# Pinned splits for late operands, one tile by token halves, and other places for the last products in a one-core encoder layer

## The chip, the core and the metric

The kernel runs on one core of a Trainium2 chip. The metric is device time in microseconds (us), the median of the runs shown. A core has five engines that matter here, each with its own instruction order: TensorE (PE; PEld is its weight load), VectorE (DVE), ScalarE (ACT), GpSimd (POOL) and SyncE (SP). SP and POOL issue DMAs; POOL's are those that add to what is in the target. Engines wait for each other through semaphores. A wait of one instruction holds everything behind it on its engine.

## The reference

One layer of an encoder, 1024 tokens by 1024 model columns in float32: a norm, a mixer (pooling and chunked attention), an output projection, a gated convolutional MLP with 2816 hidden columns, and a gated embedding. The change concerns the MLP and what follows it:

```python
    hn = rmsnorm(h, norm_ffn_g[i])
    up = hn @ w_up[i]
    gt, val = up[..., :D_FF], up[..., D_FF:]
    gt = causal_dwconv(gt, conv_w[i], conv_b[i])
    h = h + (jax.nn.gelu(gt, approximate=False) * val) @ w_down[i]
    hn = rmsnorm(h, norm_ple_g[i])
    gate = jax.nn.sigmoid(hn @ w_ple_gate[i] + b_ple_gate[i])
    h = h + gate * (p[i] @ w_ple[i])
return rmsnorm(h, final_g)
```

## The kernel before, in words

Every large product is made of three matmuls on split operands. `split` (L132) copies a 128x512 block on ACT into a reduced type (hi, L133) and subtracts that copy from the block on DVE (lo, L134); `mm3` (L126 to L130) then issues hi by hi (L128), hi by lo (L129) and lo by hi (L130).

*Up projection.* The 2816 hidden columns are 22 tiles `fi` of 128, each with a gate and a value column block. For each tile the two by two block product (gate and value columns by the two token halves) is done with seven products instead of eight, in a scheme of Strassen's kind. Product n of tile fi is written (fi,n) below; `product` makes it from 12 matmuls into a PSUM bank. The order is `steps`, n = 1, 5, 6, 2, 7, 3, 4 for most tiles; tiles 0 and 1 differ, and four products are run ahead, in the order (0,1), (1,1), (0,2), (0,5). `prepare` gets the weight operand of a product ready three products ahead: `fetch` (L695) loads w_up blocks (v,z) into one of six buffers, `summed` (L699) adds blocks on DVE where a product wants a sum, and `split` makes hi and lo. A buffer that a later sum has finished with goes to the next load, so which sums are made in place sets when loads can be issued. `step` does what follows a product: `keep` (L784) copies a bank to memory on ACT, `seed` (L788) copies one bank to another so that the next product can add to it, and DVE lines (L807 to L824) form gate and value. `gate` (L833 to L836) is the convolution and the gelu, `values_in` (L841 to L850) multiplies it by the value. A tile in `halved` has its gate done by token halves.

*Down projection.* Tiles 0 to 19 are stored to memory (L891, `Yd`), in groups of four tiles. For each of the five groups seven products (order 1, 2, 5, 4, 6, 7, 3; eight calls of `mm3`, 24 matmuls, each) are run in between up products. Their operands are sums of w_down blocks and of stored tiles; the DMA makes the sums: `ask` issues a plain load on SP (L942) and adding loads on POOL (L940) into the raw buffers RW, as far as the tiles that it needs are stored. `split_next` splits the four raw buffers (two of weights, two of activations; negative ones by L972 and L973) into the pair buffers, three of which are called BQ, and `down_next` runs the product and adds the banks to the residual (L990). `places` tells behind which up products of tile fi a down product runs.

*The last two tiles.* Tiles 20 and 21 are not stored; after tile 21 they go through a plain down product, with rows of w_down, and the embedding p and w_ple are multiplied as well. These late operands are loaded and split by `late_pair` (L1038), which has two buffers at first and six later.

The order of TensorE is that of the program. For ACT, DVE, SP and POOL a scheduler chooses the order from what is ready; `tc.high_priority(AHEAD)` lets an instruction go ahead by up to AHEAD places.

Of the kernel before, what the change touches and what calls it, by code (L numbers as in the profile page):

```python
# [12 lines left out]
SEQ = 1024  # L13
# [80 lines left out]
def trunk(tc, xT, pT, vecs, w_qk0, w_in, w_v, bias, counts, pool_w, w_out, w_up, w_down,  # L94
# [4 lines left out]
    with tc.tile_pool(name="sb", bufs=1) as sb, \  # L99
# [23 lines left out]
        def rv(ap):  # L123
            return ap.bitcast(F32)
# [4 lines left out]
            pe.matmul(ps, ahi, blo, start=False, stop=False, skip_group_check=more)  # L129
            pe.matmul(ps, alo, bhi, start=False, stop=last, skip_group_check=more)  # L130

        def split(src, hi, lo):  # L132
            act.activation(hi, src, AF.Copy)  # L133
            dve.tensor_tensor(lo, src, rv(hi), ALU.subtract)  # L134


        mhalf = small[:, 0:1]
# [530 lines left out]
        rst = f(44, SEQ)  # L668
        ahead = [(0, 1), (1, 1), (0, 2), (0, 5)]
        alone = ahead[:3]  # L670
        steps = {0: (6, 3, 7, 4), 1: (5, 6, 2, 7, 3, 4)}
        for fi in range(2, NF):
            steps[fi] = (1, 5, 6, 2, 7, 3, 4)
        order = ahead + [(fi, n) for fi in range(NF) for n in steps[fi]]
# [26 lines left out]
        def prepare(upto):  # L701
            while prepared[0] < min(upto, len(order)):
                fi, n = order[prepared[0]]
                w_ = wu[prepared[0] % 3]
                prepared[0] += 1
                fetch(prepared[0] + 3)
                assert fetched[0] == len(loads) or loads[fetched[0]][0] >= prepared[0]
                if (fi, n) in alone:
                    t, = done_with = [held[(fi, n), q] for q in FORMS[n]]
                else:  # L710
                    a11, a12, a21, a22 = [held.get((fi, q)) for q in ((0, 0), (0, 1), (1, 0), (1, 1))]
                    if n == 5:
                        summed(a21, a21, a22)
                    elif n == 6:
                        summed(a21, a21, a11)
                    elif n == 3 and not fi:
                        summed(a11, a21, a12)
                    elif n == 7:
                        if fi:
                            summed(a11, a21, a12)  # L720
                        summed(a21, a21, a22, ALU.subtract)
                    t = {1: a11, 5: a21, 2: a12, 6: a21, 3: a11, 7: a21, 4: a22}[n]
                    done_with = {3: [a11, a12], 7: [a21], 4: [a22]}.get(n, []) if fi == 0 else {
                        3: [a11], 7: [a12, a21], 4: [a22]}.get(n, [])
                with tc.high_priority(AHEAD):
                    split(rawu[t].rearrange("p (k c) -> p k c", k=4), w_[:, 0], w_[:, 1])
                for q in done_with:
                    used[q] = False
# [48 lines left out]
        p5, u2 = f(56.25, 512), f(58.25, 512)  # L777
        G2 = Gb[:, 2 + 512:2 + 1024]
        firsts = {0: (0, 3, 5, 4), 1: (2, 3, 1, 5)}
        halved = (1, NF - 1)  # L780

        def keep(dst, bank, scale=1.0):
            with tc.high_priority(AHEAD):
# [6 lines left out]
        def step(fi, n):  # L790

            x, y, z, w = firsts.get(fi, (0, 1, 2, 3))
            product({1: x, 2: x, 5: z, 3: z, 6: y, 7: y, 4: w}[n], n in (1, 5) or (fi, n) == (0, 4))
            if n == 1 and fi != 1:
                seed(y, x, -1.0)
            elif n == 2 and fi:
                gate0(x)
                if fi in halved:
                    gate(fi, HS[0])
            elif n == 5:  # L800
                keep(p5, z)
            elif n == 6:
                keep(u2, y)
            elif n == 3:
                if fi == 0:
                    norm_b.rows(rst[:, HS[1]])
                dve.tensor_tensor(G2, PS[:, z], u2, ALU.subtract)  # L807
                dve.tensor_tensor(G2, G2, rst[:, HS[1]], ALU.mult)
                gate(fi, HS[1] if fi in halved else slice(0, SEQ))
            elif n == 7:  # L810
                if fi:
                    seed(w, y)
                else:
                    keep(V[:, HS[0]], y)
                dve.tensor_tensor(V[:, HS[1]], PS[:, y], p5, ALU.subtract)
            elif n == 4:
                if fi:
                    dve.tensor_tensor(V[:, HS[0]], PS[:, w], rst[:, HS[0]], ALU.mult)
                else:
                    dve.tensor_tensor(V[:, HS[0]], PS[:, w], V[:, HS[0]], ALU.add)  # L820
                    dve.tensor_tensor(V[:, HS[0]], V[:, HS[0]], rst[:, HS[0]], ALU.mult)
# [16 lines left out]
        def values_in(ts, negative=None):  # L838
            b = max(ts.start, 512)
            if ts.stop > b:  # L840
                dve.tensor_tensor(V[:, b:ts.stop], V[:, b:ts.stop], rst[:, b:ts.stop], ALU.mult)  # L841
            if negative is None:
                dve.tensor_tensor(Yb[:, ts], Yb[:, ts], V[:, ts], ALU.mult)
                return
            for h in range(2):
                y = Yb[:, HS[h]]
                if h == negative:
                    dve.scalar_tensor_tensor(y, y, -1.0, V[:, HS[h]], ALU.mult, ALU.mult)
                else:
                    dve.tensor_tensor(y, y, V[:, HS[h]], ALU.mult)  # L850
# [26 lines left out]
        def up(fi, dst, hooks=None):  # L877
            if fi == 0:
                pool.memset(Gb[:, 0:2], 0.0)
                gate0(firsts[0][0])  # L880
            if fi == 1:
                seed(firsts[1][1], firsts[1][0], -1.0)
            for n in steps[fi]:
                step(fi, n)
                for hook in (hooks or {}).get(n, ()):
                    hook()
            if isinstance(dst, int):

                values_in(slice(0, SEQ), dst)
                for ts in HS:  # L890
                    sp.dma_start(Yd[fi][:, ts], Yb[:, ts])  # L891
                stored.add(fi)
                ask()
                if fi > 3:
                    split_next()
                return
            for ts in HS if fi % 2 else [slice(0, SEQ)]:
                values_in(ts)
                if dst is not None:
                    store(dst, ts)  # L900
# [19 lines left out]
        def ask():  # L920
# [3 lines left out]
            for side in "wa":  # L924
                for kind in ("one", "grow"):
                    queue = todo_of[side, kind]
                    while queue:
                        g, n, before = queue[0]
                        if before is not None and (side,) + before not in split_done:
                            break  # L930
                        if side == "a" and not all(group_of(g)[2 * k + j] in stored for k, _ in DOWN_A[n] for j in range(2)):
                            break
                        queue.pop(0)
                        asked.add((side, g, n))
                        grown = n in (GROWING_W if side == "w" else GROWING_A)[1:]
                        for j, srcs in sources(side, g, n):
                            t = raws[side, kind, j]
                            for z, src in enumerate(srcs):
                                if z or grown:
                                    pool.dma_start(t, src, accum_op=ALU.add)  # L940
                                else:
                                    sp.dma_start(t, src)  # L942
# [11 lines left out]
        sequence = [(g, n) for g in range(5) for n in DOWN_ORDER]  # L954
        nsplit, ndown = [0], [0]

        def split_next():
            if nsplit[0] == len(sequence) or nsplit[0] > ndown[0]:
                return
            g, n = sequence[nsplit[0]]  # L960
# [3 lines left out]
            for side in "wa":  # L964
                sign = -1.0 if side == "a" and n in NEGATIVE else 1.0
                for j in range(2):
                    t = raws[side, buffer(side, n), j]
                    hi, lo = pairs[side, j]
                    if sign > 0:
                        split(t, hi, lo)  # L970
                    else:
                        act.activation(hi, t, AF.Copy, scale=-1.0)  # L972
                        dve.scalar_tensor_tensor(lo, t, -1.0, rv(hi), ALU.mult, ALU.subtract)  # L973
# [26 lines left out]
        for fi in range(4):  # L1000
# [15 lines left out]
            if fi == 2:  # L1016
# [2 lines left out]
                                     (H[d][:, HS[1]], H[4 + d][:, HS[1]], ALU.add)):  # L1019
                        dve.tensor_tensor(a, a, b, op)  # L1020
                ask()
                split_next()
        places = [(1, 5), (2, 6), (3,), (0, 4)]
        for fi in range(4, NF - 3):
            up(fi, negative(fi), downs(fi, places[fi % 4]))
# [6 lines left out]
        pt = [[(r(b, 512), r(b + 2, 512)) for b in (96 + 16 * h, 104 + 16 * h)] for h in range(2)]  # L1032
        banks = (4, 5, 6, 7, 0, 2, 1, 3)
        nl = len(loads)
        late = [rawu[(nl + z) % 6] for z in (0, 1)]
        nlate = [0]

        def late_pair(src, hi, lo):  # L1038
            t = late[nlate[0] % len(late)]
            nlate[0] += 1  # L1040
            sp.dma_start(t, src)
            split(t, hi, lo)

        def ple_weights():
            for k in range(2):
                for z in HS:
                    late_pair(w_ple[k, :, z], wp[k][0][:, z], wp[k][1][:, z])

        def ple_rows(h):
            for k in range(2):  # L1050
                late_pair(pT[k, :, HS[h]], *pt[h][k])

        def down_weights(fi, dst):
            for z in HS:
                late_pair(w_down[fi, :, z], dst[0][:, z], dst[1][:, z])

        up(last_f[0], None, downs(last_f[0], (3, 5)))
        hooks = downs(last_f[1], (0, 2, 4, 6))
        for n, fn in ((1, lambda: store(gv2[0])), (2, ple_weights), (3, lambda: ple_rows(0)),
                      (4, lambda: late.extend(rawu[(nl + z) % 6] for z in (2, 3, 4, 5)))):  # L1060
            hooks.setdefault(n, []).insert(0, fn)
        up(last_f[1], gv2[1], hooks)
        b_pool.__exit__(None, None, None)
        b_pool = tc.tile_pool(name="po", bufs=1)
# [40 lines left out]
                mm3(PS[:, bank], wp[k][0][:, ds_], wp[k][1][:, ds_], *pt[h][k], k == 0, k == 1)  # L1105
            act.activation(po[8 * h + d], PS[:, bank], AF.Copy)

        down_weights(last_f[0], wd2[0])
        down_weights(last_f[1], wd2[1])
        ple_rows(1)  # L1110
        for d in range(KT):
            ple_mm(0, d, ple_banks[d])
        gate_weights(range(4))
# [164 lines left out]
```

## Time and profile before

| | us |
|---|---|
| runs | 1144.33, 1145.61, 1144.48 (median 1144.48) |
| profiled execution | 1146.88 |
| its span | 1145.1 |
| TensorE busy | 1129.9 |
| VectorE busy | 888.2 |
| ScalarE busy | 604.7 |
| GpSimd busy | 146.8 |

The mean granted clock of TensorE in the profiled execution is 0.995. The span is from the first to the last instruction of the profile. Matmuls overlap, so the time from one start to the next is what a matmul costs in a row; the duration in a timeline row is longer. In a row of the timeline the bracket gives the idle time ahead of the instruction and what ended it. "SPq" and "POOLq" are the queues of the engines that issue DMAs.

### The profile page before, as it was taken

How to read it: one execution, taken by the hardware profiler on the slowest of the kernel's cores; microseconds unless marked ns; L12 is line 12 of the kernel's file. 1: busy time of each engine (PE TensorE's matmuls, PEld its weight loads, DVE VectorE, ACT ScalarE, POOL GpSimd, SP SyncE). 2: the span in 40 equal slices, each digit the busy share in tenths (PEclk: the TensorE clock that was granted, in tenths of full speed). 3: DMA queues.
4: the chain of work that ended last, by engine and by line, in shares of the span. 5: the costliest groups of instructions: out<-in, count | busy, mean ns of one | idle time of the engine just before them, and what ended most of it. 6: DMA issues, size and time to landing. Idle time of an engine off the chain costs nothing.

```text
span 1145.1 us, 15750 instructions
## 1 busy us (share of the span) xinstructions
PE 1129.9 (99%) x5675; PEld 958.2 (84%) x5675; DVE 888.2 (78%) x1541; ACT 604.7 (53%) x1068; POOL 146.8 (13%) x192
## 2 busy tenths in 40 slices
PE   9999999999999999999999999999999999999997
PEld 7988998888888778888888888888888887788897
DVE  7678878879658787888787878777887788986864
ACT  8568677765554554444444444443444344664644
POOL 0000000073002200120112011201120113000000
PEclk9999999999999999999999999999999999999999
DMA  7110101104500343575557655755575559320012
GB/s 265 37 49 31 50 12 68 40 28 151 172 19 10 97 128 117 140 172 140 144 144 162 158 148 146 173 141 145 152 172 138 145 148 183 114 92 19 1 74 74
DMA packets 65022, 125.89 MB, mean 110 GB/s; under 512 B 7344, under 2 KB 8624, under 8 KB 64944
## 3 DMA queue, kind: packets, MB, share of 16 engines
q1 hardware_dynamic: 50400, 98.60, 25.9%
q0 software_dynamic: 14400, 26.22, 14.1%
q8 instruction: 44, 0.72, 0.3%
q14 instruction: 34, 0.28, 0.1%
q10 hardware_dynamic: 144, 0.07, 0.0%
HBM read 110.18 MB, written 14.68 MB: 109 GB/s over the span
## 4 chain that ended last, share of the span: by engine, by line
PE 93%; issue 2%; ACT 2%; DMA 1%; DVE 1%; SPq 0%; POOL 0%; POOLq 0%; DVEq 0%; ACTq 0%
PE PS L128 28%; PE PS L129 28%; PE PS L130 28%; PE PS L367 2%; PE PS L385 1%; PE PS L384 1%; DMA F<-in_w_down 1%; PE PS L342 1%; PE PS L341 1%; DMA F<-in_w_qk 0%; PE PS L350 0%; PE PS L349 0%; PE PS L617 0%; DMA RW<-in_w_down 0%; ACT F L353 0%
## 5 line engine op out<-in xcount | busy, mean ns | idle before, releaser
L128 PE MATMUL PS<-R 128*128 128x512 f32 (+1 forms) x1176 | 443.2, 377 | 2.8 <-ACT F L784 2.1
L130 PE MATMUL PS<-R 128*128 128x512 f32 (+1 forms) x1176 | 438.4, 373 | 0.0
L129 PE MATMUL PS<-R 128*128 128x512 f32 (+1 forms) x1112 | 420.8, 378 | 0.3 <-DVE R L230 0.3
L128 PEld LDWEIGHTS PS<-R 128*128 128x128 f32 x1176 | 222.1, 189 | 40.7 <-ACT F L784 2.8
L130 PEld LDWEIGHTS PS<-R 128*128 128x128 f32 x1176 | 222.1, 189 | 39.1
L129 PEld LDWEIGHTS PS<-R 128*128 128x128 f32 x1112 | 210.0, 189 | 37.1 <-DVE R L230 0.9
L133 ACT ACTIVATE R<-F 128x512 fp32r<-128x512 f32 (+2 forms) x225 | 141.3, 637 | 186.1 <-PE PS L129 76.4
L134 DVE TENSOR_TENSOR R<-F,R 128x512 fp32r<-128x512 f32 (+2 forms) x221 | 152.8, 699 | 53.2 <-ACT R L133 52.3
L133 ACT ACTIVATE BQ<-RW 128x512 fp32r<-128x512 f32 x90 | 52.8, 623 | 85.5 <-PE PS L129 78.8
L990 DVE TENSOR_TENSOR F<-F,PS 128x512 f32<-128x512 f32 x140 | 92.3, 680 | 4.4 <-PE PS L130 4.3
L699 DVE TENSOR_TENSOR F<-F 128x512 f32<-128x512 f32 x88 | 60.5, 687 | 44.1 <-DMA F<-in_w_up 41.0
L940 POOL DMA_DIRECT2D RW<-Yd x60 | 52.4, 873 | 267.2 <-DMA RW<-Yd 215.2
L940 POOL DMA_DIRECT2D RW<-in_w_down x40 | 36.1, 951 | 227.1 <-DMA RW<-in_w_down 190.1
L134 DVE TENSOR_TENSOR BQ<-RW,BQ 128x512 fp32r<-128x512 f32 x90 | 59.1, 684 | 5.6 <-ACT BQ L133 4.3
L129 PE MATMUL PS<-BQ 128*128 128x512 f32 x140 | 54.9, 392 | 2.7 <-DVE BQ L973 2.7
L353 ACT ACTIVATE F<-F,small 128x640 f32<-128x640 f32 (+2 forms) x64 | 44.4, 693 | 21.1 <-DVE small L351 13.1
L128 PE MATMUL PS<-BQ 128*128 128x512 f32 x140 | 54.8, 392 | 0.3 <-ACT BQ L972 0.3
L128 PE MATMUL PS<-R,BQ 128*128 128x512 f32 x140 | 55.0, 393 | 0.0
L129 PE MATMUL PS<-R,BQ 128*128 128x512 f32 x140 | 54.9, 392 | 0.0
L130 PE MATMUL PS<-BQ 128*128 128x512 f32 x140 | 54.8, 391 | 0.0
L130 PE MATMUL PS<-R,BQ 128*128 128x512 f32 x140 | 54.7, 391 | 0.0
L609 ACT ACTIVATE F<-F 128x512 f32<-128x512 f32 (+1 forms) x49 | 27.9, 569 | 44.6 <-DVE F L1145 16.7
(186 smaller groups left out, 1803.0 us busy)
## 6 DMA issues: line engine op xcount, KB each, us to landing
F<-in_w_up SPq DMA_DIRECT2D x91, 256.0 KB, 4.2
RW<-Yd SPq DMA_DIRECT2D x60, 256.0 KB, 3.7
RW<-Yd POOLq DMA_DIRECT2D x60, 256.0 KB, 5.1
RW<-in_w_down SPq DMA_DIRECT2D x50, 256.0 KB, 2.8
RW<-in_w_down POOLq DMA_DIRECT2D x40, 256.0 KB, 6.2
Yd<-F SPq DMA_DIRECT2D x40, 256.0 KB, 2.4
F<-in_w_in SPq DMA_DIRECT2D x10, 512.0 KB, 3.5
F<-in_xT SPq DMA_DIRECT2D x16, 256.0 KB, 5.8
```

The lines of the kernel that those rows point to most:

```text
L128: pe.matmul(ps, ahi, bhi, start=first, stop=False, skip_group_check=more)
L129: pe.matmul(ps, ahi, blo, start=False, stop=False, skip_group_check=more)
L130: pe.matmul(ps, alo, bhi, start=False, stop=last, skip_group_check=more)
L133: act.activation(hi, src, AF.Copy)
L134: dve.tensor_tensor(lo, src, rv(hi), ALU.subtract)
L341: pe.matmul(PS[:, 4 + z, 0:320], q, K2[:, ks], start=True, stop=False)
L353: act.activation(S[:, 0:n], S[:, 0:n], AF.Exp, bias=s_[:, 0:1], scale=-1.0, accum_out=s_[:, 1:2])
L367: pe.transpose(pst[:, j * P:(j + 1) * P], S[:, j * P:(j + 1) * P], ident)
L609: act.activation(self.q, src, AF.Square)
L699: dve.tensor_tensor(rawu[to], rawu[a], rawu[b], op)
L940: pool.dma_start(t, src, accum_op=ALU.add)
L990: dve.tensor_tensor(t, t, PS[:, 4 + d], ALU.subtract if n in (1, 5) else ALU.add)
```

## The change

`split` can pin its two instructions to the program's order. The first `split_next` (in tile 2) and the late splits use this.

```diff
-        def split(src, hi, lo):
-            act.activation(hi, src, AF.Copy)
-            dve.tensor_tensor(lo, src, rv(hi), ALU.subtract)
+        def split(src, hi, lo, pinned=False):
+            both = (act.activation(hi, src, AF.Copy),
+                    dve.tensor_tensor(lo, src, rv(hi), ALU.subtract))
+            if pinned:
+                for i in both:
+                    tc.keep_in_program_order(i)
...
-                split_next()
+                split_next(True)
```

Tile 1 gets another order of products, and the sums, flags and the kept copy of tile 0. Tile 19 (NF - 3) is added to the halved tiles, and its values, stores and `ask` run by token halves; what is stored is kept by tile and half.

```diff
-        steps = {0: (6, 3, 7, 4), 1: (5, 6, 2, 7, 3, 4)}
+        steps = {0: (6, 3, 7, 4), 1: (5, 2, 6, 3, 7, 4)}
...
-                    elif n == 3 and not fi:
+                    elif n == 3 and fi < 2:
                         summed(a11, a21, a12)
                     elif n == 7:
-                        if fi:
+                        if fi > 1:
                             summed(a11, a21, a12)
                         summed(a21, a21, a22, ALU.subtract)
...
-        halved = (1, NF - 1)
+        halved = (1, NF - 3, NF - 1)
...
             elif n == 7:
-                if fi:
+                if fi > 1:
                     seed(w, y)
                 else:
                     keep(V[:, HS[0]], y)
...
-                values_in(slice(0, SEQ), dst)
-                for ts in HS:
-                    sp.dma_start(Yd[fi][:, ts], Yb[:, ts])
-                stored.add(fi)
-                ask()
+                for part in [HS[0:1], HS[1:2]] if fi == NF - 3 else [HS]:
+                    values_in(slice(part[0].start, part[-1].stop), dst)
+                    for ts in part:
+                        sp.dma_start(Yd[fi][:, ts], Yb[:, ts])
+                        stored.add((fi, HS.index(ts)))
+                    ask()
```

The late operands become a list of twelve pieces with a buffer each in a fixed order; they are split, pinned, in four lots behind products 5, 6, 7 and 4 of tile 21. Calls that did this after tile 21 or in other places are gone. The last group's down products run behind other up products.

```diff
-        late = [rawu[(nl + z) % 6] for z in (0, 1)]
...
+        late = [rawu[(nl + z) % 6] for z in (0, 1, 5, 3, 2, 0, 1, 5, 3, 4, 2, 0)]
+        pieces = []
+        for z, fi in enumerate(last_f):
+            pieces += [(w_down[fi, :, ts], wd2[z][0][:, ts], wd2[z][1][:, ts]) for ts in HS]
+        pieces += [(pT[k, :, HS[0]], *pt[0][k]) for k in range(2)]
+        for k in range(2):
+            pieces += [(w_ple[k, :, ts], wp[k][0][:, ts], wp[k][1][:, ts]) for ts in HS]
+        pieces += [(pT[k, :, HS[1]], *pt[1][k]) for k in range(2)]
...
+        def late_pairs(n):
+            for _ in range(n):
+                src, hi, lo = pieces[npiece[0]]
+                t = late[npiece[0]]
+                npiece[0] += 1
+                sp.dma_start(t, src)
+                split(t, hi, lo, True)
...
-        up(last_f[0], None, downs(last_f[0], (3, 5)))
-        hooks = downs(last_f[1], (0, 2, 4, 6))
-        for n, fn in ((1, lambda: store(gv2[0])), (2, ple_weights), (3, lambda: ple_rows(0)),
-                      (4, lambda: late.extend(rawu[(nl + z) % 6] for z in (2, 3, 4, 5)))):
-            hooks.setdefault(n, []).insert(0, fn)
+        up(last_f[0], None, downs(last_f[0], (2, 4, 6)))
+        hooks = downs(last_f[1], (1, 3, 5))
+        hooks.setdefault(1, []).insert(0, lambda: store(gv2[0]))
+        for n, many in ((5, 2), (6, 4), (7, 4), (4, 2)):
+            hooks.setdefault(n, []).insert(0, lambda many=many: late_pairs(many))
...
-        down_weights(last_f[0], wd2[0])
-        down_weights(last_f[1], wd2[1])
-        ple_rows(1)
```

The number of matmuls is the same. ACT has two instructions more and DVE three more; the DMAs are the same in number. Line numbers of the changed file are up to 18 higher: L784 and L788 become L787 and L791, L699 becomes L702, L833 to L836 become L836 to L839, L972 and L973 become L978 and L979, L940 and L942 become L946 and L948, and the late splits' loads are at L1056.

More of the change, by code (lines that the diff above doesn't have):

```diff
@@ L722, in prepare @@
                     t = {1: a11, 5: a21, 2: a12, 6: a21, 3: a11, 7: a21, 4: a22}[n]
-                    done_with = {3: [a11, a12], 7: [a21], 4: [a22]}.get(n, []) if fi == 0 else {
+                    done_with = {3: [a11, a12], 7: [a21], 4: [a22]}.get(n, []) if fi < 2 else {
                         3: [a11], 7: [a12, a21], 4: [a22]}.get(n, [])
@@ L792, in step @@
             x, y, z, w = firsts.get(fi, (0, 1, 2, 3))
-            product({1: x, 2: x, 5: z, 3: z, 6: y, 7: y, 4: w}[n], n in (1, 5) or (fi, n) == (0, 4))
+            product({1: x, 2: x, 5: z, 3: z, 6: y, 7: y, 4: w}[n], n in (1, 5) or n == 4 and fi < 2)
             if n == 1 and fi != 1:
@@ L816, in step @@
             elif n == 4:
-                if fi:
+                if fi > 1:
                     dve.tensor_tensor(V[:, HS[0]], PS[:, w], rst[:, HS[0]], ALU.mult)
@@ L845, in values_in @@
             for h in range(2):
+                if HS[h].stop <= ts.start or HS[h].start >= ts.stop:
+                    continue
                 y = Yb[:, HS[h]]
@@ L930, in ask @@
                             break
-                        if side == "a" and not all(group_of(g)[2 * k + j] in stored for k, _ in DOWN_A[n] for j in range(2)):
+                        if side == "a" and not all((group_of(g)[2 * k + j], t) in stored for k, t in DOWN_A[n] for j in range(2)):
                             break
@@ L955, in trunk, with split_next @@
         nsplit, ndown = [0], [0]
-        def split_next():
+        def split_next(pinned=False):
             if nsplit[0] == len(sequence) or nsplit[0] > ndown[0]:
@@ L969, in split_next @@
                     if sign > 0:
-                        split(t, hi, lo)
+                        split(t, hi, lo, pinned)
                     else:
@@ L1034, in trunk @@
         nl = len(loads)
-        late = [rawu[(nl + z) % 6] for z in (0, 1)]
[L1036 to L1055, printed above, removed]
-        up(last_f[0], None, downs(last_f[0], (3, 5)))
-        hooks = downs(last_f[1], (0, 2, 4, 6))
-        for n, fn in ((1, lambda: store(gv2[0])), (2, ple_weights), (3, lambda: ple_rows(0)),
-                      (4, lambda: late.extend(rawu[(nl + z) % 6] for z in (2, 3, 4, 5)))):
-            hooks.setdefault(n, []).insert(0, fn)
+        late = [rawu[(nl + z) % 6] for z in (0, 1, 5, 3, 2, 0, 1, 5, 3, 4, 2, 0)]
[6 more added lines that the diff above has]
+        pieces += [(pT[k, :, HS[1]], *pt[1][k]) for k in range(2)]
+        npiece = [0]
+        def late_pairs(n):
[10 more added lines that the diff above has]
+            hooks.setdefault(n, []).insert(0, lambda many=many: late_pairs(many))
         up(last_f[1], gv2[1], hooks)
```

## The prediction

> **What bounds the kernel now.** I read the page first, then the waits of TensorE, then the chain of waits and the windows around each wait. The page's head gives the bound:
>
> ```profile
> span 1145.1 us, 15750 instructions
> ...
> PE 1129.9 (99%) x5675; PEld 958.2 (84%) x5675; DVE 888.2 (78%) x1541; ACT 604.7 (53%) x1068; POOL 146.8 (13%) x192
> ```
>
> TensorE is busy for 99% of the span and its instruction count does not change, so the change can only win what TensorE now loses to waits and to a lower clock. The waits (engine, line, releaser: us in total, times, longest):
>
> ```profile
> PE PS L129 <- DVE BQ L973: 2.7, 2, 1.6
> ...
> PE PS L128 <- ACT F L784: 2.1, 1, 2.1
> ...
> PE PS L128 <- ACT PS L788: 0.7, 1, 0.7
> PE PS L128 <- ACT BQ L972: 0.3, 1, 0.3
> ```
>
> Five waits, 5.8 us, all on splits, copies and seeds whose order the change moves. The windows say where the rest goes (time, then busy us and count of PE, PEld, DVE, ACT, POOL, then PEclk, DMA share, GB/s):
>
> ```profile
> 393.30:396.70 3.40, 1.32 (x8) 0.94 (x7) 1.29 (x2) 1.95 (x4) 0.00 (x0) 0.99 0.83 282
> 396.70:400.10 3.40, 3.40 (x9) 2.62 (x9) 3.14 (x7) 1.85 (x4) 1.98 (x2) 0.51 0.86 271
> ...
> 412.90:948.70 535.80, 535.80 (x2366) 443.65 (x2365) 428.47 (x656) 234.75 (x378) 78.29 (x90) 1.00 0.58 148
> ...
> 953.10:956.50 3.40, 2.27 (x10) 1.56 (x9) 2.40 (x5) 2.08 (x4) 0.04 (x1) 1.00 0.78 142
> 977.00:980.40 3.40, 1.48 (x5) 0.67 (x4) 3.40 (x7) 3.29 (x7) 0.00 (x0) 0.99 0.00 0
> 980.40:983.80 3.40, 3.40 (x9) 2.63 (x8) 3.40 (x6) 1.29 (x2) 0.00 (x0) 0.51 0.33 104
> ```
>
> From 412.9 to 948.7 TensorE never stops; the losses lie in two places, tiles 0 and 1 (391 to 413) and the last two tiles (949 to 998). A stretch of 3.4 us in which TensorE was busy for 1.32 or 1.48 us is followed by one at clock 0.51, while one with 2.27 is not. The chain of waits at both places (start, us, what):
>
> ```profile
> 390.89 3.75 DMA RW<-in_w_down
> ...
> 395.81 0.59 ACT F L784
> 396.44 0.63 PE PS L128
> ...
> 400.05 0.29 PE PS L130
> 400.35 0.23 PE PS L128
> ...
> 403.63 0.63 ACT R L133
> ...
> 405.57 1.06 ACT F L836
> ...
> 407.17 0.50 PE PS L128
> ```
>
> ```profile
> 954.82 0.69 DVE BQ L973
> 955.55 0.50 PE PS L129
> ...
> 967.79 8.20 DMA F<-in_w_down
> ...
> 979.83 0.50 PE PS L129
> 980.65 0.43 PE PS L128
> ...
> 983.63 0.34 PE PS L129
> ```
>
> Here (f,n) is product n of up tile f, or of down group 4. A matmul takes 0.227 us in a row (the 0.23 at 400.35).
> (0,7): 2.08 idle, since the first down group's weight split stands on ACT ahead of u2's copy L784 and waits for its load until 394.64. Then nine matmuls run from 396.44 to 400.34, 3.90 where 2.04 would do: 1.86. Together 3.94.
> (1,6): 0.68 for the seed L788, and 0.50 for a matmul instead of 0.23: 0.95.
> (4,4): 1.13 and 0.27 for the restart: 1.40.
> (4,7): 0.33 + 1.59, then ten matmuls from 979.83 to 983.97, 4.14 instead of 2.27: 3.79. ACT stood 8.20 us at a late w_down split, with the splits of (4,7) behind it.
> Sum: 10.08 us to win at most.
>
> **The change part by part.** *Pinned first split* (split_next(True) in tile 2). The first group's four splits go behind tile 2's own work on ACT and DVE, some 40 us later; their product runs in tile 4 alone. This removes (0,7)'s 3.94: (0,7) starts at 394.36 and (1,5) ends 3.94 earlier than the 406.49 (407.17 - 0.68) of before, at 402.55.
>
> *Order of tile 1 and its sums.* The changed order runs (1,2) where (1,6) stood, right after (1,5). It still waits for the seed, which now reads the bank that (1,2) adds to. What is late next is a load: w_up block (0,0) of tile 1 is asked for after block (0,1), and on SP it now stands behind tile 0's last needed w_up load and four w_down loads.
>
> ```profile
> 392.42 4.04 SPq L942 DMA_DIRECT2D RW<-in_w_down  x3
> ...
> 399.35 1.41 DVE L699 TENSOR_TENSOR F<-F 128x512 f32<-128x512 f32 x2
> ...
> 402.54 1.28 DVE L835 SCALAR_TENSOR_TENSOR F<-F,vec 128x1024 f32<-128x1024 f32 x1
> ```
>
> ```profile
> F<-in_w_up SPq DMA_DIRECT2D x91, 256.0 KB, 4.2
> ```
>
> It can be issued at about 393.4, when its buffer is free (two 0.5 us issues after 392.42). With the page's 4.2 us it lands at 397.6. As sixth of a queue whose first landed at 394.64 (390.89 + 3.75), each 256 KB at 271 GB/s taking 0.97, it lands at 399.5. I take the middle, 398.6. The sum L699 (two of them, 1.41) waits for it and stands on DVE ahead of tile 0's gate L834 and L835, and the gelu, the seed and (1,2) wait for these. In before this run of DVE work lasted from 399.35 to 403.82, 4.47 us; from 398.6 it ends at 403.1. Gelu to matmul took 407.17 - 405.57 = 1.60, so (1,2) starts at 404.7, 2.2 after (1,5) ends. If the load is in time, the old limit holds: ACT's split at 403.63 to 407.17 is 3.54, counted from a product boundary, and the wait stays 0.68. The late end (399.5) makes it 3.1. I take 2.2, with 0.27 for the restart 2.5. TensorE runs before and after it; split on the 3.4 us stretches found above (396.7, 400.1, 403.5, 406.9), 1.0 of the idle falls in one and 1.2 in the next, each leaving at least 2.2 busy, like the stretch at 953.10 that cost no clock. So this place goes from 3.94 + 0.95 to 2.5.
>
> *Seed replaced by a kept copy for tile 1, halved tiles, two more ACT and three more DVE instructions.* They lie in tiles 1 and 19, where DVE has idle time (428.47 of 535.80 busy), and cost nothing there; without that cover, 5 times 0.7, 3.5 us.
>
> *Down products one place earlier in the last tiles* ((2,4,6) and (1,3,5) for (3,5) and (0,2,4,6)). Each moves one product, 12 x 0.227 = 2.72, ahead, so its operands must come earlier too. For (4,2), fed by tile 19:
>
> ```profile
> 908.08 0.69 DVE L699 TENSOR_TENSOR F<-F 128x512 f32<-128x512 f32 x1 [4.23 <-DMA F<-in_w_up]
> ...
> 924.40 0.69 DVE L848 SCALAR_TENSOR_TENSOR F<-F,V 128x512 f32<-128x512 f32 x1
> ```
>
> ```profile
> 927.35 0.38 SPq L942 DMA_DIRECT2D RW<-Yd  x1
> ```
>
> ```profile
> 931.50 0.63 ACT L972 ACTIVATE R<-RW 128x512 fp32r<-128x512 f32 x1 [2.06 <-DMA RW<-Yd]
> ```
>
> ```profile
> 932.16 0.69 DVE L973 SCALAR_TENSOR_TENSOR R<-RW,R 128x512 fp32r<-128x512 f32 x1 [2.01 <-ACT R L972]
> ```
>
> ```profile
> 932.28 0.39 PE L128 MATMUL PS<-BQ 128*128 128x512 f32 x1
> ```
>
> Before, (4,2) started at 932.28, and its last operand was ready at 932.85, when its fifth matmul wanted it (932.28 + 0.91 = 933.19): no slack beyond 0.3. Now it starts at 929.56. The token halves gain little: DVE cannot begin before 908.08, a load, and is packed from there; counted in the changed order the first half of Y ends about 0.4 earlier, at 924.7. From Y's end (925.09) to the operand took 7.76, with two stores and two other loads between; the new order puts one load between store and reload instead, up to 0.7 less. So it is ready at 931.7 to 932.4, and the fifth matmul wants it at 930.47: a wait of 1.2 to 1.9, of which I take 1.4 and 0.27 for the restart, 1.7. (All times here are those of before; what the first place saves shifts work and loads alike.)
>
> (4,4) moves the same 2.72 ahead, 1.7 of it covered by (4,2)'s wait, so its wait lies between 0 (if its accumulating loads, chained on POOL, start earlier with it) and 1.40 + 2.72 - 1.7 = 2.4 (if not). One more accumulate now stands on POOL ahead of the chain that ends last. I take 0.6, near the lower end, as the halves are stored before it. (4,6) comes 48 matmuls, 10.9 us, after (4,4), and between their last operands stand 18 DVE instructions, two of them wide: 16 x 0.60 + 2 x 1.2 = 12.0 to 12.3. Wait 0 to 1.4; I take 1.0.
>
> *Late operands.* Their twelve loads are written next to their splits, in four lots (2, 4, 4, 2) behind steps 5, 6, 7 and 4 of tile 21. Each load is issued when its buffer is free, in the changed order some 20 us ahead of its split for the first two (the slowest took 8.20); the least room has the second w_down half of tile 21, a rival below. ACT's splits of (4,7) no longer stand behind one, so (4,7)'s 3.79 goes. The work of ACT and DVE is the same, and in 998 to 1046 it falls out of a stage where TensorE never waits.
>
> *Sum.* After: 2.5 + 1.7 + 0.6 + 1.0 = 5.8, from 10.08: 4.3 saved. The profiled execution took 1146.88 with a span of 1145.1, 2.40 over the median of the runs, 1144.48; so 1146.88 - 4.3 = 1142.6 for such an execution and 1140.2 for the median.
>
> The Trainium skill, "TensorE: Matmul & The Clock Gate", Part 1 (The HAM clock gate), says that half rate follows an idle window of about 3.4 us. Here the clock fell after idle spells of 2.08 and 1.92, so the measurement decides: by the page no wait of this kernel would cost clock, and the sum would gain 3.7 less.
>
> **The rivals.**
> *Half clock after a wait.* The new waits are 2.2 and 1.4 long. If either lies whole within one stretch, that has 1.2 to 2.0 busy, near the 1.48 that was followed by 0.51, and 1.87 is lost. For: two of five waits were followed so. Against: my placing of the stretches. Time 1140.2 + 1.9 = 1142.1; twice, 1143.9. The same page's section says that the windows run free of the kernel's start, which would make the placing differ from run to run.
> *All loads in time.* The w_up load lands by 397.2 and the operands of (4,2) to (4,6) come one place earlier with them. Then only 0.95 stays: 9.1 saved, 1135.4. Against: the reload of tile 19 was only just in time before.
> *The waits only change place.* Landing at 399.5 (3.1), (4,2) 1.9, (4,4) 2.4, (4,6) 1.4 and half clock once make about 10.9 with restarts: 1144 to 1145.3.
> *Slower: a pinned split becomes the wait.* ACT and DVE must now keep the written order at the twelve late splits.
>
> ```profile
> 962.00:974.00 12.00, 12.00 (x55) 9.94 (x54) 6.96 (x11) 3.34 (x6) 3.49 (x4) 1.00 0.99 199
> ```
>
> With the DMA engines 0.99 busy, the load for the last tile's second w_down half is issued near 968 and, with 8.20, lands at 976; behind its split stand the splits of (4,3) and tile 21's gate, some 10 us of DVE work before a product due near 988. So (4,3) waits for whatever lands after 977, plus 1.87 for the clock. The change is slower by 0.2% (2.3 us) from a landing after 977 + 10.1 + 2.3 - 5.8 - 1.9 = 981.7, nearly 14 us after issue; landing at 984 gives 1144.48 - 10.1 + 5.8 + 7 + 1.9 = 1149.1. Against: no load took over 8.20.
> *The pins don't hold* and the 3.94 stays: about 1144.
>
> **How the numbers follow.** The forecast has 0.38; half clock 0.22; all in time 0.14; waits that change place or pins that don't hold 0.13; slower 0.13. This kernel's measurement tells 0.2%, 2.3 us, from no change: faster is below 1142.2. That holds for 0.36 of the forecast, 0.11 of half clock and all 0.14: 0.61. Same: 0.25. Slower: 0.14. The range leaves out the slower rival and half of "all in time": 1135.4 to 1145.5.
>
> **What would show it.** Right: no wait on L784's successor (u2) in tile 0 and no chain step of w_down there; one wait of about 2.2 at tile 1's second product, released by the seed (now L791); short waits on BQ near 927, 951 and 962; no wait at (4,7) and PEclk 1.00 there. Wrong: a clock of 0.51 after any of them, a chain through F<-in_w_down or in_pT past 960, or (4,2)'s wait over 2.5.

## The result and the profile after

| | before | changed |
|---|---|---|
| median of the runs, us | 1145.01 (10 runs) | 1150.09 (10 runs) |
| lowest and highest | 1142.95, 1147.67 | 1147.51, 1154.42 |
| profiled execution | 1146.88 | 1151.44 |
| its span | 1145.1 | 1149.6 |

The ratio of the changed kernel to the one before is 1.0046, 95% interval 1.0031 to 1.0060: some 5 us slower, where 4.3 us faster was forecast. The measured median lies above the upper end of the forecast, 1145.5.

The waits of TensorE in the changed kernel (engine, line, releaser: us in total, times, longest):

```profile
PE PS L128 <- ACT R L978: 6.9, 2, 4.7
PE PS L128 <- ACT PS L791: 2.2, 1, 2.2
...
PE PS L128 <- ACT R L232: 0.9, 1, 0.9
```

None of the five waits of before is left as it was. The 2.1 at (0,7) and the pair at (4,7) are gone, and so is (4,4)'s 1.1 for its first activation operand. There are three new ones: 2.2 for the seed, as forecast for (1,2); and two behind ACT's L978, the copy of a negative activation operand, of 2.2 at (4,2) and of 4.7 at (4,4). The 0.9 at L232 is in the first 10 us, before anything that the change touches. The other kernels below show between nothing (e1, and before) and 1.9 there, and it is counted to none of the changes; it makes every later time of this profile 0.9 later.

The windows of the changed kernel (columns as in the prediction):

```profile
401.00:414.00 13.00, 10.77 (x48) 8.59 (x47) 11.05 (x17) 6.58 (x10) 0.00 (x0) 1.00 0.61 155
414.00:926.00 512.00, 511.88 (x2258) 423.53 (x2258) 411.76 (x633) 225.57 (x364) 71.68 (x82) 1.00 0.58 148
926.00:938.00 12.00, 9.57 (x41) 7.32 (x41) 5.63 (x10) 4.40 (x9) 0.86 (x1) 1.00 0.70 209
...
952.00:968.00 16.00, 11.28 (x37) 8.43 (x36) 9.08 (x13) 4.62 (x7) 4.95 (x6) 0.79 0.85 165
968.00:1001.00 33.00, 33.00 (x147) 27.35 (x146) 32.57 (x53) 19.60 (x35) 1.76 (x2) 1.00 0.44 118
```

Of these rows three hold nearly all the loss: 401 to 414, 926 to 938, and 952 to 968, where the clock fell to 0.79 too; from 414 to 926 it is 0.12. From 968 to 1001 TensorE never stops. How long the product (4,4) took is read from TensorE's timeline, its first matmul, the one that waited, and the first matmul after the product:

```profile
953.34 0.39 PE L128 MATMUL PS<-BQ 128*128 128x512 f32 x1
...
958.90 0.80 PE L128 MATMUL PS<-R,BQ 128*128 128x512 f32 x1 [4.72 <-ACT R L978]
...
966.84 0.40 PE L128 MATMUL PS<-R 128*128 128x512 f32 x1
```

It took 966.84 - 953.34 = 13.50 instead of 24 x 0.227 = 5.44: 8.06 lost, 4.72 of them idle and the rest at about half clock. (4,2) lost 3.0 in the same reading, (1,2) 2.5 (2.23 idle and the restart). Together 13.6 against 10.1 of before: 3.5 more. With the 0.9 of the start that is 4.4 of the 4.5 between the two spans.

The chain of waits of the changed kernel shows why (4,4) was late:

```profile
938.85 5.60 DMA RW<-Yd
...
951.71 6.40 DMA RW<-Yd
...
958.22 0.64 ACT R L978
```

And POOL's timeline, first of before, then of the changed kernel (start, us, what, idle before and what ended it):

```profile
933.42 0.86 POOL L940 DMA_DIRECT2D RW<-Yd  x1 [26.86 <-DMA RW<-Yd]
936.08 0.86 POOL L940 DMA_DIRECT2D RW<-Yd  x1 [1.80 <-issue]
939.90 0.89 POOL L940 DMA_DIRECT2D RW<-Yd  x1 [2.96 <-DMA RW<-Yd]
941.46 0.88 POOL L940 DMA_DIRECT2D RW<-Yd  x1 [0.67 <-DMA RW<-Yd]
944.18 0.86 POOL L940 DMA_DIRECT2D RW<-Yd  x1 [1.85 <-issue]
944.79 1.15 POOL L940 DMA_DIRECT2D RW<-in_w_down  x1
946.55 0.88 POOL L940 DMA_DIRECT2D RW<-Yd  x1 [0.61 <-issue]
```

```profile
932.75 0.86 POOL L946 DMA_DIRECT2D RW<-Yd  x1 [28.83 <-DMA RW<-Yd]
938.25 1.78 POOL L946 DMA_DIRECT2D RW<-Yd  x2 [4.63 <-DMA RW<-Yd]
942.44 0.87 POOL L946 DMA_DIRECT2D RW<-Yd  x1 [2.42 <-DMA RW<-Yd]
945.07 0.86 POOL L946 DMA_DIRECT2D RW<-Yd  x1 [1.75 <-DMA RW<-Yd]
945.67 1.15 POOL L946 DMA_DIRECT2D RW<-in_w_down  x1
948.19 0.88 POOL L946 DMA_DIRECT2D RW<-in_w_down  x1 [1.37 <-DVE F L996]
950.15 0.87 POOL L946 DMA_DIRECT2D RW<-Yd  x1 [1.08 <-DVE BQ L134]
951.71 0.86 POOL L946 DMA_DIRECT2D RW<-Yd  x1 [0.69 <-issue]
```

Each of the two activation operands of (4,4) is a load and three adds, one after the other, since each add needs the sum so far. Before, POOL issues them in turn: first operand, second, first, second (933.42, 936.08, 939.90, 941.46), and the second operand's last add at 946.55. In the changed kernel the first operand's second add stands right behind its first. It cannot be issued until that has landed (932.75 to 938.25, with POOL idle for 4.63), and the second operand's first add, which is ready, waits behind it on POOL: it goes at 938.85 instead of 936.08. The loss is handed on: its second add goes at 945.07 instead of 941.46 and takes 4.8 us to land, until 949.8. Its last add then stands behind one for the next product, which waits for a split of DVE and goes at 950.15: 951.71 instead of 946.55, of which this last place is about 1.5 (the two adds of w_down ahead of it had gone by then). With 6.40 to land, ACT gets the operand at 958.22. Before, it was 952.08:

```profile
952.08 0.63 ACT L972 ACTIVATE R<-RW 128x512 fp32r<-128x512 f32 x1 [2.46 <-DMA RW<-Yd]
```

The product now also stands one place, 2.7 us, earlier in TensorE's order.

### The profile page after: what moved, and what is told of

Its sections match the earlier page's. It is cut to its first block, busy times and chain, and to the rows that moved or that the text cites. A ratio compares the mean times of both kernels' runs of the same rounds, so it can differ in the third digit from the quotient of the medians.

```text
span 1149.6 us, 15757 instructions
## 1 busy us (share of the span) xinstructions
PE 1129.6 (98%) x5675; PEld 957.2 (83%) x5675; DVE 888.7 (77%) x1544; ACT 604.8 (53%) x1070; POOL 146.6 (13%) x192
## 4 chain that ended last, share of the span: by engine, by line
PE 84%; DVE 5%; issue 3%; DMA 3%; ACT 2%; POOL 1%; SPq 0%; POOLq 0%; DVEq 0%; ACTq 0%
PE PS L128 26%; PE PS L129 26%; PE PS L130 25%; PE PS L370 2%; DVE R L134 2%; DMA RW<-Yd 1%; PE PS L388 1%; PE PS L387 1%; DMA F<-in_w_up 1%; PE PS L345 1%; PE PS L344 1%; DMA F<-in_w_v 1%; ACT R L133 0%; PE PS L353 0%; POOL RW L946 0%
## 5 line engine op out<-in xcount | busy, mean ns | idle before, releaser
L702 DVE TENSOR_TENSOR F<-F 128x512 f32<-128x512 f32 x88 | 60.5, 687 | 51.6 <-DMA F<-in_w_up 48.7
L946 POOL DMA_DIRECT2D RW<-Yd x60 | 52.8, 885 | 269.9 <-DMA RW<-Yd 219.6
L946 POOL DMA_DIRECT2D RW<-in_w_down x40 | 36.1, 962 | 226.1 <-DMA RW<-in_w_down 186.0
L836 ACT ACTIVATE F<-F,vec 128x1024 f32<-128x1024 f32 (+1 forms) x25 | 28.6, 1143 | 46.4 <-DVE F L811 44.0
```

Source lines behind the costliest of these rows:

```text
L702: dve.tensor_tensor(rawu[to], rawu[a], rawu[b], op)
L836: act.activation(y, Gb[:, 2 + a:2 + b], AF.Identity, bias=vec[:, C_CB + fi:C_CB + fi + 1], scale=cw(2))
```

## The experiments

Theory A: POOL's order, which the scheduler chose anew, made (4,4) late. Theory B: the products stand one place too early. Theory C: the late operands' loads crowd the DMA engines. Ratios are to the kernel before, with 95% intervals; the median beside each is of its own runs.

### Order of POOL's adds (e1)

```diff
-                        for j, srcs in sources(side, g, n):
-                            t = raws[side, kind, j]
-                            for z, src in enumerate(srcs):
+                        both = [(raws[side, kind, j], srcs) for j, srcs in sources(side, g, n)]
+                        for z in range(len(both[0][1])):
+                            for t, srcs in both:
                                 if z or grown:
-                                    pool.dma_start(t, src, accum_op=ALU.add)
+                                    i = pool.dma_start(t, srcs[z], accum_op=ALU.add)
+                                    if g == 4:
+                                        tc.keep_in_program_order(i)
                                 else:
-                                    sp.dma_start(t, src)
+                                    sp.dma_start(t, srcs[z])
```

> The changed kernel with one thing different: the adding loads of the last group are written pair by pair and pinned on POOL, so that the second activation operand of (4,4) is no longer queued behind the second add of the first operand, nor its last add behind two w_down adds. Theory A (POOL's queue order made (4,4) late): its last add is issued near 948 instead of 951.7 and lands near 952 to 953 instead of 958.1; the wait at (4,4) falls from 4.7 to 0.5 or less, the half clock behind it goes, and the time falls by about 7.5 us, to about 1142.6. Theory B (the product is simply one place too early): wait of 2 or more stays, time 1147 or more. Theory C (the late operands' loads crowd the DMA engines): the adds still take over 6 us each and the wait stays above 3.

Measured: 0.9983 (0.9970 to 0.9995), 1143.88 us. POOL's timeline of this kernel:

```profile
932.68 0.86 POOL L946 DMA_DIRECT2D RW<-Yd  x1 [25.49 <-DMA RW<-Yd]
935.46 0.86 POOL L946 DMA_DIRECT2D RW<-Yd  x1 [1.91 <-issue]
...
945.80 0.86 POOL L946 DMA_DIRECT2D RW<-Yd  x1 [1.68 <-issue]
946.41 1.17 POOL L946 DMA_DIRECT2D RW<-in_w_down  x1
```

and its ACT's, and its windows over the two places of the last tiles where the changed kernel lost time:

```profile
950.68 0.63 ACT L980 ACTIVATE R<-RW 128x512 fp32r<-128x512 f32 x1 [0.60 <-DMA RW<-Yd]
```

```profile
926.00:938.00 12.00, 10.04 (x37) 7.58 (x36) 5.94 (x10) 3.18 (x6) 1.73 (x2) 0.86 0.75 205
...
952.00:968.00 16.00, 16.00 (x72) 13.24 (x72) 15.09 (x23) 8.83 (x14) 6.12 (x7) 1.00 0.95 193
```

The last add is issued at 945.80 and the operand is there at 950.68, before the product. TensorE has no idle time from 952 to 968, at full clock, although the DMA engines are busier there (0.95) than in the changed kernel (0.85). Places, halves and late loads are as in the changed kernel, so theory A holds, and B and C fall as the main cause: the order on POOL alone is worth 0.63% (1.0046 to 0.9983), 7 us. What this profile still loses is elsewhere: 2.6 at (1,2) and 1.8 at (4,2), each with a stretch of half clock behind it (the 0.86 above is that of (4,2)).

### Without the token halves (e2)

```diff
-        halved = (1, NF - 3, NF - 1)
+        halved = (1, NF - 1)
...
-                for part in [HS[0:1], HS[1:2]] if fi == NF - 3 else [HS]:
+                for part in [HS]:
```

> The changed kernel without tile 19's token halves (values, stores and requests of the whole tile at once, as before). POOL's order then alternates between the two operands again. Theory A: the wait at (4,4) falls below 1, while that at (4,2) grows by 0.4 to 1.0, to about 2.6 to 3.4; time about 1143.5 to 1145. Theories B and C: the wait at (4,4) stays at 4 or more, and the time is 1150 or more.

Measured: 0.9999 (0.9987 to 1.0010), 1147.02 us: 0.47% less than the changed kernel, but above the 1143.5 to 1145 that A expected. The adds go in turn again, and the wait at (4,4) is 1.9: less than half of 4.7, but not the 1 or less expected. The second operand's second and last adds:

```profile
941.67 0.87 POOL L946 DMA_DIRECT2D RW<-Yd  x1 [1.52 <-DMA RW<-Yd]
...
949.81 0.87 POOL L946 DMA_DIRECT2D RW<-Yd  x1 [0.27 <-issue]
```

They took 6.7 and 6.3 us to land, against 4.6 and 4.8 in e1. So how long an add takes is part of this wait, besides POOL's order; what made these two slow is not shown. An add of w_down at 948.66 also stood ahead of the last one, about 1 us. (4,2) waited 1.4 in this profile, not the 2.6 to 3.4 expected, and (1,2) 3.1, with half clock behind it.

### The old places (e3)

```diff
-        up(last_f[0], None, downs(last_f[0], (2, 4, 6)))
-        hooks = downs(last_f[1], (1, 3, 5))
+        up(last_f[0], None, downs(last_f[0], (3, 5)))
+        hooks = downs(last_f[1], (0, 2, 4, 6))
```

> The changed kernel with the last group's products at their places of before ((3,5) in tile 20, (0,2,4,6) in tile 21); the halves, the pins and tile 1 as changed. Theory B: no wait at (4,2), at most 1.4 at (4,4), no half clock, time about 1139 to 1141. Theory A: no wait at (4,2), but (4,4) still waits 2 to 3 us, since the second operand's adds are still queued behind the first's; time about 1142 to 1144. Theory C: as A or worse, with adds of over 6 us.

Measured: 1.0034 (1.0018 to 1.0050), 1150.61 us. No wait at (4,2), but 6.3 at (4,4), half clock behind it, 0.5 and 1.2 at (4,7), and 3.2 at (1,2). POOL's timeline:

```profile
933.95 0.86 POOL L946 DMA_DIRECT2D RW<-Yd  x1 [24.41 <-DMA RW<-Yd]
940.33 1.78 POOL L946 DMA_DIRECT2D RW<-Yd  x2 [5.52 <-DMA F<-in_w_down]
...
952.08 0.86 POOL L946 DMA_DIRECT2D RW<-Yd  x1 [3.87 <-DMA RW<-Yd]
```

POOL's order is that of the changed kernel (two adds together at 940.33), and the last add goes out at 952.08. (The bracket of 940.33 names the last of several landings, here a late load's at 940.1; the first operand's first add, of 933.95, took 6.0 us, until 939.9.) Putting the products back does not help while the operand is this late; theory B is wrong. A expected this wait at 2 to 3 and the time at 1142 to 1144, so A's numbers were missed: it had not counted that the last add, too, would be issued as late as in the changed kernel (952.08).

### The halves alone (e9)

The kernel before with tile 19's part of the change (`halved`, the loop over `part`, what is stored kept by half), nothing else.

> The kernel before with tile 19's token halves alone (and what is stored kept by half); places, late operands, tile 1 and pins as before. If the halves alone put the second operand of (4,4) behind the first on POOL, its last add lands near 958 instead of 952 and (4,4) waits 4 to 6.5 us instead of 1.1, with half clock behind it: ratio 1.003 to 1.006. If it takes the other parts too (the late loads on SP, the places), the wait stays near 1.1 and the ratio is 1.000.

Measured: 1.0045 (1.0030 to 1.0060), 1150.41 us. POOL's timeline of it:

```profile
934.58 0.86 POOL L943 DMA_DIRECT2D RW<-Yd  x1 [22.34 <-DMA RW<-Yd]
939.49 1.78 POOL L943 DMA_DIRECT2D RW<-Yd  x2 [4.05 <-DMA F<-in_w_ple]
...
951.34 0.86 POOL L943 DMA_DIRECT2D RW<-Yd  x1 [4.11 <-DMA RW<-Yd]
```

The halves alone turn POOL's order round, and alone they cost as much as the whole change: 0.45% here, and the 0.47% that e2 gained without them. The profiled execution (1147.79, where the runs go from 1147.06 to 1155.35) waited only 1.7 at (4,4), less than the 4 to 6.5 expected: its last add took 4.4 us to land, against 6.4 in the changed kernel. So this profile does not itself show where the median's loss lies; that slower landings lengthen the wait in the other runs, as in the changed kernel, is not shown.

### The sum of (1,6) (e4)

```diff
-                        summed(a21, a21, a11)
+                        i = summed(a21, a21, a11)
+                        if fi == 1:
+                            tc.keep_in_program_order(i)
```

(`summed` returns its instruction.)

> The changed kernel with the sum of (1,6) pinned on DVE, so that it stands behind tile 0's gate. If the late w_up load holds the gate and so the seed, the wait at (1,2) falls from 2.2 to about 0.7 and the rest stays: 1.5 us less, about 1148.6. If something else holds the seed (the gelu table load, the order of ACT), the wait stays at about 2.2.

Measured: 1.0011 (1.0000 to 1.0022), 1147.89 us. DVE in the changed kernel, and in this one:

```profile
399.68 1.42 DVE L702 TENSOR_TENSOR F<-F 128x512 f32<-128x512 f32 x2 [2.82 <-DMA F<-in_w_up]
401.02 1.28 DVE L837 SCALAR_TENSOR_TENSOR F<-F,vec 128x1024 f32<-128x1024 f32 x1
```

```profile
399.85 1.28 DVE L839 SCALAR_TENSOR_TENSOR F<-F,vec 128x1024 f32<-128x1024 f32 x1 [1.31 <-ACT F L838]
...
403.45 0.68 DVE L702 TENSOR_TENSOR F<-F 128x512 f32<-128x512 f32 x1
```

In the changed kernel DVE stood 2.82 us at the sum, for the w_up load, with the gate behind it. With the sum pinned the gate goes first, and the wait at (1,2) is 0.3: less than the 0.7 that the prediction took for the old limit. The wait at (4,4) stays at 4.7. The time fell by 0.35%, 4 us, more than the 2 us of that wait; in this profile (4,2) waited only 0.2 as well, but it varies between 0.2 and 2.2 over the profiles of the changed order, so this extra is not shown to come from the pin.

### Both pins (e5), and (4,2) one place later (e7)

e5 is e1 with e4's pin; e7 is e5 with (3, 4, 6) for (2, 4, 6) in tile 20.

> The changed kernel with POOL's adds in pairs (as in e1) and the sum of (1,6) pinned (as in e4). If the two losses are independent they add: e1's 0.9983 and about 0.3% of e4, so about 0.995 of before, 1140.5 us; no wait over 1 at (1,2) and at (4,4), and what is left is (4,2). If one wait only hides the other, the time stays at e1's, 0.998.

> e5 with (4,2) alone back at its place of before (behind the fourth product of tile 20; the others stay one place early). If (4,2)'s wait is only its reload, it goes, about 2 us less than e5, 0.993. If (4,5), now one up product behind (4,2), waits for its pair buffers in turn, the wait moves there and the time is that of e5.

Measured: e5 0.9952 (0.9934 to 0.9970), 1140.42 us; e7 0.9949 (0.9932 to 0.9967), 1139.85 us. Both beat both kernels. The windows of e5 over the two places:

```profile
391.00:414.00 23.00, 22.68 (x101) 18.12 (x100) 18.77 (x29) 13.38 (x21) 2.22 (x3) 1.00 0.67 196
926.00:1001.00 75.00, 74.77 (x329) 61.19 (x328) 68.11 (x105) 41.33 (x68) 14.02 (x16) 1.00 0.69 168
```

0.32 and 0.23 idle, clock 1.00: in this profile next to nothing is left to wait for at the two places. The gains add up as expected. e7 is not distinguishable from e5, where (4,2) waited only 0.2; in e7 (4,5) waits, 0.5.

### The right order at the old places (e6)

e1 with e3's edit.

> e1 with the last group's products at their places of before. With POOL's order mended, the places can be judged alone. If one place earlier costs (4,2) its wait of 1.8 and gains nothing, this run has no wait at (4,2) nor at (4,4) and is 2 us faster than e1, 0.9965. If the earlier places are what keeps ACT and DVE ahead of (4,7), this run gets a wait there (e3 showed 0.5 and 1.2) and is as slow as e1 or slower, 0.998 to 1.001.

Measured: 1.0011 (0.9999 to 1.0022), 1146.68 us: slower than e1. (4,4) has no wait, but (4,7) has 0.9 and 1.2, and half clock behind them. ACT's timeline:

```profile
966.09 0.62 ACT L133 ACTIVATE R<-F 128x512 fp32r<-128x512 f32 x1
971.56 0.63 ACT L133 ACTIVATE R<-F 128x512 fp32r<-128x512 f32 x1 [4.84 <-DMA F<-in_w_down]
974.25 1.16 ACT L133 ACTIVATE R<-F 128x512 fp32r<-128x512 f32 x2 [2.06 <-DMA F<-in_pT]
975.31 1.13 ACT L133 ACTIVATE BQ<-RW 128x512 fp32r<-128x512 f32 x2
```

ACT stands 4.84 and 2.06 us at pinned splits of late operands, with the splits of (4,7), from 975.31 on, behind them. That is the mechanism of the prediction's slower rival, though at (4,7) and not at (4,3). So the pin on the late splits does not by itself remove (4,7)'s loss; with the places one up product earlier it is gone, and in e1 ACT makes these splits from 970.21 on.

### The first pin (e8 and e10)

e8 is the changed kernel with `split_next()` instead of `split_next(True)`; e10 is the kernel before with that pin alone.

> The changed kernel with the first group's split not pinned. If the pin is what removed the wait at (0,7) and its half clock, about 2.1 us of wait and a clock near 0.5 come back there; the wait at (1,2) then shrinks, since the late load has 4 us more. Time: 1.5 to 3.9 more than the changed kernel, ratio 1.006 to 1.008. If the pin does nothing, ratio 1.0046 and no wait at (0,7).

> The kernel before with the first group's split pinned, and nothing else. If the prediction's price of (0,7) holds, its wait of 2.1 and the half clock go, and the time falls by up to 3.9 us (0.9966); (1,6) keeps a wait near 0.7. If the wait only moves to the seed of (1,6), whose gate is held by a load as in the changed kernel, the wait there grows to 2 or more and the ratio is 0.998 to 1.000.

Measured: e8 1.0055 (1.0036 to 1.0074), 1151.15 us; e10 0.9990 (0.9975 to 1.0005), 1143.43 us. In e8 the wait at (0,7) is back (1.8) and that at (1,2) is 1.6 instead of 2.2, as expected; the loss of clock behind (0,7) is not, and by its time e8 cannot be told from the changed kernel. In e10 the wait at (0,7) is gone, and the one for the seed is 1.4, twice that of before and between the two cases expected. e10's profiled execution took 1140.92, and its runs go up to 1148.28, so the size is not settled: something between nothing and 0.25%, less than the 3.9 us (0.34%) of the prediction.

## Why the prediction was wrong, point by point

- **What bounds the kernel.** Right: TensorE's waits and clock at two places, and the change moved time nowhere else (511.88 of 512.00 busy from 414 to 926). The 10.08 to win were those of one execution, though, 2.40 slower than the median; e5 and e7, whose profiles have almost none of them left, are 5 to 6 us faster than before in the median.
- **The sum.** 5.8 was forecast to be left, and the profile has 13.6. Of the 7.8 more, 7.5 are (4,4), 1.3 are (4,2), and (4,6) gave 1.0 back.
- **(0,7) loses its wait.** Right in the profile. The price of 3.94 was that of an execution in which half clock followed; e8 has the wait without it.
- **(1,2) waits for the late w_up load, 2.2.** Right in size and in cause: 2.23, and e4 shows the chain of load, sum, gate and seed. With the 0.9 of the start taken off, the load landed at 398.7, where the prediction took 398.6, the middle of two estimates. That the clock held, as forecast, was luck: the stretches did not lie where the prediction put them (last section), and in e1, e2, e3 and e6, with waits of 2.0 to 3.2 at this place, it fell.
- **(4,2), 1.4 of idle time.** Low for this profile: 2.2 and 0.2, more than the upper bound of 1.9. In e4, e5 and e8 it is 0.2: it goes with how long the reload of tile 19 on SP takes in an execution, 5.0 and 5.4 us in the changed kernel and e1 (waits of 2.2 and 1.8), 3.9 to 4.2 in those three.
- **(4,4), 0.6.** This is the step that failed. It named the added accumulate "on POOL ahead of the chain that ends last", and priced it near the lower end "as the halves are stored before it". What was missed is that this accumulate waits for a DMA of its own (5.5 us, 932.75 to 938.25), and holds everything behind it on POOL; that each later add inherits the delay; and that the last add then stands behind one for the next product. The wait was 4.72, the loss with the clock 8.06, and the upper bound of 2.4 was too low too, since it took the landing time of before as the latest possible. e1 gave back 0.63% by that order alone; e9 brought the loss of time into the kernel before by the halves alone. The token halves, for whose sake the prediction stayed near the lower end, were what turned the order round.
- **(4,6), 1.0.** Not seen. (4,4)'s wait gave its operands time here, but in e1 and e5, where (4,4) does not wait, it is not seen either: the term was too high.
- **(4,7) keeps no wait.** Right, but the pins, to which the prediction gave this, do not do it alone: at the old places it waits in spite of them (e6). Whether the new places would do without the pins, no run shows.
- **Rivals.** The slower rival had the right sign and a wrong mechanism for the changed kernel; its mechanism was met in e6 at the old places. Half clock after a wait came too, but behind (4,4) and not behind (1,2) or (4,2), the waits that this rival had in mind. The case "all loads in time" was forecast at 1135.4; e5 and e7, which have nearly no wait left, reach 0.995 of before, about 1139.5.

What stays open: why the scheduler groups the adds by operand when the tile is stored by halves, what makes an add take 4.4 us to land in one execution and over 6 in another, and how much of the median's 5 us each wait has in an average execution; profiles are single executions, and (4,2) and (4,4) differ by 2 to 4 us between them.

## What to carry to other kernels

Storing an operand's parts earlier is a gain only if the queue that carries the next step still serves the chains in turn: after any edit of when requests are made, read the order on each DMA-issuing engine, and ask of each issue what it waits for and who stands behind it. An add into a buffer that waits for the add before it should not stand ahead of a ready one of another chain. A bound that takes "no later than before" for a landing time is no bound if the queue ahead of it has changed.

## What the runs showed of the hardware

The clock of TensorE does not follow the length of an idle spell alone. At (1,2), the changed kernel was idle for 2.23 and kept its clock; e6 was idle there for 2.05 and lost it. The windows of the changed kernel, then of e6:

```profile
401.84:405.26 3.42, 1.66 (x8) 1.04 (x6) 3.42 (x6) 1.86 (x3) 0.00 (x0) 1.00 0.90 173
405.26:408.67 3.41, 2.94 (x13) 2.43 (x14) 3.41 (x7) 1.44 (x3) 0.00 (x0) 1.00 0.07 27
```

```profile
403.30:406.70 3.40, 1.35 (x6) 0.86 (x5) 3.40 (x6) 2.57 (x4) 0.00 (x0) 1.00 0.49 124
406.70:410.10 3.40, 3.40 (x9) 2.62 (x8) 2.76 (x5) 0.14 (x1) 0.00 (x0) 0.50 0.42 123
```

In e6 the clock fell a whole microsecond after the wait had ended (405.67), at 406.71, for 3.4 us. The slow stretches lie on a grid of 3.413: their starts at 406.71 and 980.15 in e6 are 168 such steps apart, those at 396.65 and 980.33 in before 171. In the changed kernel the grid is laid back from its slow stretch behind (4,4), 958.21 to 965.04, which is an estimate. A border then falls at 405.26, inside the wait (403.50 to 405.73), and the stretches on its two sides are busy for 1.66 and 2.94; in e6 the whole wait fell into one stretch, busy for 1.35. So where a wait falls on the grid counts besides its length. How much busy time keeps the clock is not settled: it fell after a stretch with 1.60 (e1, 928.33 to 931.74) and one with 1.74 (e6, 976.74 to 980.15), and held after one with 1.54 (e2, 953.46 to 956.87). The grid agrees with the Trainium skill, "TensorE: Matmul & The Clock Gate", Part 1 (The HAM clock gate), that windows of 3413 ns run free of the kernel; that section's condition of an idle window does not agree, as 1.35 busy of 3.4 was enough to lose the clock.
